# Seven block products in a decoder trunk: gate outputs in two tiles of one bank, value outputs in one tile of two banks

## The chip, the core and the metric

The kernel runs on one core of a Trainium2 chip, as one program. The metric is the device time of one execution in microseconds (us); of several runs the median is taken.

## What is computed

Two layers of a causal decoder over 256 positions of width 2048, in fp32. Layer 0 has stick-breaking attention, layer 1 dilated sliding-window attention; both have the same feed-forward block, where the change lies:

```python
def conv_ffn(h, w_up, conv_w, conv_b, w_down):
    u = causal_depthwise_conv(h @ w_up, conv_w, conv_b)     # width 3, along the positions
    gate, val = u[..., :D_FF], u[..., D_FF:]                # D_FF = 5632
    return (jax.nn.silu(gate) * val) @ w_down
...
for i in range(DEPTH):                                      # DEPTH = 2
    h = rms_norm(x, attn_norm_w[i])
    x = x + (mixer_a(...) if i < 1 else mixer_b(...))
    x = x + conv_ffn(rms_norm(x, ffn_norm_w[i]), ffn_w_up[i], ...)
    gate = jax.nn.sigmoid(rms_norm(x, ple_norm_w[i]) @ ple_w_gate[i])
    x = x + gate * (p[i] @ ple_w_proj[i])
return rms_norm(x, final_norm_w)
```

## The kernel before

**Matmuls.** Tokens are stationary (two tiles of 128), weights are the moving operand, 512 columns (a strip) at a time. Each operand is split into a high and a low part in a reduced fp32 format, and a block product is three matmuls: low tokens by high weights, high by low, high by high (`add_block`, lines 342 to 344). So a tile of weights, two blocks of 128 rows by 512 columns, gives 12 matmuls: two blocks, two token tiles, three matmuls.

**Weights.** `weights` loads four blocks (1 MB) at a time into `raw` (four buffers, SyncE's queue), then ScalarE (ACT) makes the high part `whi` of two blocks (line 305) and VectorE (DVE) the low part `wlo` (line 306). Four buffers of each are there, so the split runs up to four tiles ahead of TensorE (PE).

**Outputs in PSUM.** The eight banks of PSUM are dealt out by tag: "acc", a ring of five tiles of one bank; "att", one tile of one bank; "two", one tile of two banks. A strip's output is two banks, one for each token tile. `scaled` (line 540) copies them out on ScalarE, two transposes on VectorE (line 243) and a trip through memory (lines 246 and 254, GpSimd's queue) turn them, and the convolution runs on the turned strip (lines 905 to 914).

**Seven products.** In the up projection the strips come in pairs, each with a gate strip and a value strip. For every second pair, four of the 16 blocks of rows are taken out of the strips and made as one two by two block product (two token tiles by the gate and the value strip), with seven products instead of eight, ahead of the pair. `Seven` holds this: `load` fetches the two strips' weights, `first` to `seventh` each issue six matmuls (line 455) on weights that `parts` splits (lines 445 and 446). The outputs are four banks: c11 and c21 belong to the next gate strip (`strip_among` goes on accumulating into them), c12 and c22 to the next value strip. The first four products run between the weight tiles of the value strip before (`HEADS8`, `HEADS6`), the fourth ahead of its last tile. Then VectorE combines the outputs in place:

```python
def fourth(self):
    ...
    nc.vector.tensor_tensor(self.p, self.c22, self.p, op=OP.add)        # line 495
    nc.vector.tensor_tensor(self.c21, self.c21, self.p, op=OP.add)      # line 496
    nc.vector.tensor_tensor(self.c22, self.q, self.c21, op=OP.subtract) # line 497
    nc.vector.tensor_tensor(self.c12, self.c12, self.p, op=OP.subtract) # line 498
```

The other three products run within the next gate strip (`TAILS`): the fifth, into c11, ahead of its first weight tile; the sixth, into c21, ahead of the second; the seventh, into c12, ahead of the fourth. A weight tile gives six matmuls into the first bank, then six into the second. There are ten such blocks of seven: two and three in the two parts of each layer's feed-forward.

**What sets the order.** A scheduler places the instructions of each engine by priority and by its own estimate of time, and each engine then runs its list in order. It also sets the waits, and it tracks accesses by tile: an instruction that writes one bank of a tile of two banks waits for instructions that use the other. `high_priority` moves the weight splits and the combining steps forward in VectorE's and ScalarE's lists.

Of the kernel before, what the change touches and what calls it, by code (L numbers as in the profile page):

```python
# [75 lines left out]
def tile_trunk(ctx, tc, head_d, xT_d, x_d, pT_d, pos_d, vec_d, cst_d, csb_d, wqkv, wo_a, wkv, wq_b, wo_b, wup, wdn, wpg, wpp, gfin_d, out_d):  # L76
# [11 lines left out]
    def nm(s):  # L88
        uid[0] += 1
        return f"{s}_{uid[0]}"  # L90

    def bank(s, tag="att"):
        return psum.tile([P, 512], F32, tag=tag, bufs=NBANK[tag], name=nm(s))

    def two_banks():
        return psum.tile([P, 2, 512], F32, tag="two", bufs=1, name=nm("two"))
# [4 lines left out]
    def tt(s, shape=(P, S), dt=F32, tag=None, bufs=None):  # L101
        kw = {} if bufs is None else {"bufs": bufs}
        return tmp.tile(list(shape), dt, tag=tag or s, name=nm(s), **kw)
# [235 lines left out]
    def add_block(ps, x, t, hi, lo, first, final, again=False):  # L339
        xh = x[:, t * P : (t + 1) * P]  # L340
        xl = x[:, S + t * P : S + (t + 1) * P]
        nc.tensor.matmul(ps, xl, hi, start=first, stop=False, skip_group_check=again)  # L342
        nc.tensor.matmul(ps, xh, lo, start=False, stop=False, skip_group_check=again)  # L343
        nc.tensor.matmul(ps, xh, hi, start=False, stop=final, skip_group_check=again)  # L344
# [82 lines left out]
    class Seven:  # L427
# [36 lines left out]
            (self.b11, self.b21), (self.b12, self.b22) = ((r[:, :2], r[:, 2:]) for r in raws)  # L464

        def first(self):
            gates = two_banks()
            self.c11, self.c21 = gates[:, 0], gates[:, 1]
            self.c12, self.c22 = (bank("seven", "acc") for _ in range(2))
            both = tt("part", (P, 1024), tag="e", bufs=1)  # L470
            self.p, self.q = both[:, :512], both[:, 512:]
            w = self.parts(self.b11)
            self.t, self.u = self.b11, self.b12
            self.add(self.t, self.b11, self.b12)
            self.add(self.u, self.b12, self.b22)
            self.product(self.c11, self.token(0, 0), w, True)
            with tc.high_priority(offset=AHEAD):
                nc.scalar.activation(self.p, self.c11, AF.Copy)
# [162 lines left out]
    def stick_weights(q, k):  # L641
# [41 lines left out]
        return [ws[1 - h // 2][:, h % 2 * 3 : h % 2 * 3 + 3] for h in range(HG)]  # L683

    def mixer_a(xs, rc, first):
        ring_room = lambda: rt("u")
        rq = tt("rq", (P, 2), bufs=2)
# [502 lines left out]
```

## Time and profile before

| | |
|---|---|
| median of 3 runs | 2318.47 us (2317.86 to 2318.61) |
| the profiled execution | 2320.84 us, span from first to last instruction 2319.1 us |
| TensorE busy | 2285.9 us, 99% |
| VectorE busy | 1624.0 us, 70% |
| ScalarE busy | 1300.0 us, 56% |
| mean granted clock of TensorE | 0.993 |
| moved by DMA | 538.44 MB, mean 232 GB/s |

Shares are of the span. A matmul's row has the time from its start to its modelled end, drain included, so matmuls overlap: of two in a row the distance of the starts says what one costs. The granted clock is the share of full speed that TensorE was given. A name such as `two<-whi,h` reads: output tile, then the inputs.

### The profile page before, as it was taken

How to read it: one execution, taken by the hardware profiler on the slowest of the kernel's cores; microseconds unless marked ns; L12 is line 12 of the kernel's file. 1: busy time of each engine (PE TensorE's matmuls, PEld its weight loads, DVE VectorE, ACT ScalarE, POOL GpSimd, SP SyncE). 2: the span in 40 equal slices, each digit the busy share in tenths (PEclk: the TensorE clock that was granted, in tenths of full speed). 3: DMA queues.
4: the chain of work that ended last, by engine and by line, in shares of the span. 5: the costliest groups of instructions: out<-in, count | busy, mean ns of one | idle time of the engine just before them, and what ended most of it. 6: DMA issues, size and time to landing. Idle time of an engine off the chain costs nothing.

```text
span 2319.1 us, 27960 instructions
## 1 busy us (share of the span) xinstructions
PE 2285.9 (99%) x10137; PEld 1890.0 (81%) x10137; DVE 1624.0 (70%) x2335; ACT 1300.0 (56%) x1734; POOL 328.7 (14%) x575
## 2 busy tenths in 40 slices
PE   9999999999999999999999999999999999999998
PEld 7888888877888778788888888887788877878887
DVE  7666666788756788865677765778875578886565
ACT  6554555666534666645565554666653466664554
POOL 0211111111100111101011331211110011110100
PEclk9999999999999999999999999999999999999999
DMA  8877677676755767757676776768675577776763
GB/s 295 260 236 249 218 246 242 224 255 214 246 200 182 250 224 237 260 206 243 213 256 241 253 260 216 257 227 265 221 249 195 186 245 227 240 256 205 242 227 118
DMA packets 98347, 538.44 MB, mean 232 GB/s; under 512 B 16672, under 2 KB 17568, under 8 KB 46752
## 3 DMA queue, kind: packets, MB, share of 16 engines
q1 hardware_dynamic: 63360, 435.46, 54.2%
q0 software_dynamic: 32560, 95.98, 13.6%
q10 hardware_dynamic: 2288, 5.21, 0.6%
q8 instruction: 79, 1.29, 0.2%
q14 instruction: 60, 0.49, 0.1%
HBM read 486.52 MB, written 50.07 MB: 231 GB/s over the span
## 4 chain that ended last, share of the span: by engine, by line
PE 96%; DVE 2%; ACT 1%; DMA 1%; issue 0%; POOL 0%
PE accv L343 25%; PE accv L344 25%; PE accv L342 25%; PE two L342 3%; PE two L343 3%; PE two L344 3%; PE two L455 3%; PE seven L344 2%; PE seven L342 2%; PE seven L343 2%; PE two L554 1%; PE seven L455 1%; ACT whi L305 1%; DVE wlo L306 1%; DVE wlo L446 0%; DMA turned<-there 0%
## 5 line engine op out<-in xcount | busy, mean ns | idle before, releaser
L306 DVE TENSOR_TENSOR wlo<-raw,whi 128x1024 fp32r<-128x1024 f32 (+1 forms) x784 | 952.0, 1216 | 573.9 <-ACT whi L305 571.5
L305 ACT ACTIVATE whi<-raw 128x1024 fp32r<-128x1024 f32 (+1 forms) x784 | 825.7, 1054 | 808.2 <-PE accv L344 619.3
L342 PE MATMUL accv<-whi,h 128*128 128x512 f32 (+1 forms) x1688 | 655.6, 389 | 2.5 <-ACT whi L305 1.7
L344 PE MATMUL accv<-whi,h 128*128 128x512 f32 (+1 forms) x1688 | 657.0, 389 | 0.0
L343 PE MATMUL accv<-wlo,h 128*128 128x512 f32 (+1 forms) x1688 | 656.1, 389 | 0.0
L342 PEld LDWEIGHTS accv<-whi,h 128*128 128x128 f32 x1688 | 317.3, 188 | 68.6 <-ACT whi L305 2.2
L343 PEld LDWEIGHTS accv<-wlo,h 128*128 128x128 f32 x1688 | 317.3, 188 | 65.7 <-DVE wlo L306 0.4
L344 PEld LDWEIGHTS accv<-whi,h 128*128 128x128 f32 x1688 | 317.4, 188 | 64.8
L246 POOL DMA_DIRECT2D there<-y x162 | 91.7, 567 | 1300.2 <-DVE y L243 1282.4
L342 PE MATMUL accv<-whi,g 128*128 128x512 f32 x704 | 273.9, 389 | 0.0
L343 PE MATMUL accv<-wlo,g 128*128 128x512 f32 x704 | 273.9, 389 | 0.0
L344 PE MATMUL accv<-whi,g 128*128 128x512 f32 x704 | 273.9, 389 | 0.0
L254 POOL DMA_DIRECT2D turned<-there x324 | 190.1, 594 | 449.7 <-DMA there<-y 202.7
L343 PEld LDWEIGHTS accv<-wlo,g 128*128 128x128 f32 x704 | 132.2, 188 | 27.5
L342 PEld LDWEIGHTS accv<-whi,g 128*128 128x128 f32 x704 | 132.2, 188 | 27.5
L344 PEld LDWEIGHTS accv<-whi,g 128*128 128x128 f32 x704 | 132.2, 188 | 27.2
L445 ACT ACTIVATE whi<-raw 128x1024 fp32r<-128x1024 f32 x70 | 74.0, 1058 | 63.2 <-PE accv L344 35.5
L446 DVE TENSOR_TENSOR wlo<-raw,whi 128x1024 fp32r<-128x1024 f32 x70 | 85.5, 1221 | 26.3 <-ACT whi L445 26.3
L342 PE MATMUL two<-whi,h 128*128 128x512 f32 x240 | 96.1, 400 | 0.0
L343 PE MATMUL two<-wlo,h 128*128 128x512 f32 x240 | 95.5, 398 | 0.0
L344 PE MATMUL two<-whi,h 128*128 128x512 f32 x240 | 95.1, 396 | 0.0
L342 PE MATMUL seven<-whi,h 128*128 128x512 f32 x240 | 93.4, 389 | 0.0
(206 smaller groups left out, 2441.5 us busy)
## 6 DMA issues: line engine op xcount, KB each, us to landing
raw<-in_wup SPq DMA_DIRECT2D x176, 1024.0 KB, 5.4
raw<-in_wdn SPq DMA_DIRECT2D x88, 1024.0 KB, 5.0
there<-y POOLq DMA_DIRECT2D x171, 256.0 KB, 5.3
turned<-there POOLq DMA_DIRECT2D x324, 128.0 KB, 4.9
raw<-in_wqkv SPq DMA_DIRECT2D x40, 1024.0 KB, 6.0
raw<-in_wpg SPq DMA_DIRECT2D x32, 1024.0 KB, 4.9
raw<-in_wkv SPq DMA_DIRECT2D x24, 1024.0 KB, 5.3
raw<-in_wo_a SPq DMA_DIRECT2D x16, 1024.0 KB, 5.3
```

The source lines that it names most:

```text
L246: nc.gpsimd.dma_start(there[t * P : (t + 1) * P], y)
L254: nc.gpsimd.dma_start(z[32 * b : 32 * b + 32].rearrange("p a o r -> p a (o r)"), back[b])
L305: last["high"] = nc.scalar.activation(hi[:, c], r, AF.Copy).ins
L306: last["low weights"] = nc.vector.tensor_tensor(lo[:, c], r, f32(hi[:, c]), op=OP.subtract).ins
L342: nc.tensor.matmul(ps, xl, hi, start=first, stop=False, skip_group_check=again)
L343: nc.tensor.matmul(ps, xh, lo, start=False, stop=False, skip_group_check=again)
L344: nc.tensor.matmul(ps, xh, hi, start=False, stop=final, skip_group_check=again)
L445: last["high"] = nc.scalar.activation(hi, r, AF.Copy).ins
L446: last["low weights"] = nc.vector.tensor_tensor(lo, r, f32(hi), op=OP.subtract).ins
L455: nc.tensor.matmul(ps, x, y, start=begins, stop=ends, skip_group_check=True)
L554: run.append(nc.tensor.matmul(*args, skip_group_check=True, **kw).ins)
```

## The change

c11 and c21, the gate outputs, become two tiles of one bank: c11 in the bank of tag "att", c21 in the ring "acc". c12 and c22, the value outputs, become the tile of two banks, tag "two". Nothing else is edited.

```diff
         def first(self):
-            gates = two_banks()
-            self.c11, self.c21 = gates[:, 0], gates[:, 1]
-            self.c12, self.c22 = (bank("seven", "acc") for _ in range(2))
+            self.c11, self.c21 = bank("gates"), bank("gates", "acc")
+            values = two_banks()
+            self.c12, self.c22 = values[:, 0], values[:, 1]
```

TensorE's instructions keep their order, as do the queues of SyncE and GpSimd; only waits differ on TensorE, while VectorE's and ScalarE's lists change near the block products. The rows below are from the first block, and the others read the same. A number behind a name tells one tile from another; in brackets stand the engines and queues that a row waits for.

TensorE at the end of the value strip, before (the fifth product begins in the third row, with weights 3849 and 3850):

```order
L343 MATMUL accv_3618<-wlo_3798,h_3318 128x512
L344 MATMUL accv_3618<-whi_3797,h_3318 128x512
L455 MATMUL two_3641<-whi_3849,h_2700 128x512 [waits DVE_49,Activation_49]
L455 MATMUL two_3641<-wlo_3850,h_2700 128x512
L455 MATMUL two_3641<-whi_3849,h_2700 128x512
```

And now:

```order
L343 MATMUL accv_3618<-wlo_3798,h_3318 128x512
L344 MATMUL accv_3618<-whi_3797,h_3318 128x512
L455 MATMUL gates_3641<-whi_3849,h_2700 128x512 [waits Activation_49]
L455 MATMUL gates_3641<-wlo_3850,h_2700 128x512 [waits DVE_49]
L455 MATMUL gates_3641<-whi_3849,h_2700 128x512
```

Before, the first row of the product held a wait for VectorE that covered all that follows; now that row waits for ScalarE's high part alone and the second for the low part.

TensorE six matmuls later, now, in the first weight tile of the gate strip:

```order
L342 MATMUL gates_3641<-whi_3861,h_2862 128x512 [waits Activation_49]
L343 MATMUL gates_3641<-wlo_3862,h_2862 128x512 [waits DVE_49]
L344 MATMUL gates_3641<-whi_3861,h_2862 128x512
L342 MATMUL gates_3641<-whi_3861,h_2865 128x512
L343 MATMUL gates_3641<-wlo_3862,h_2865 128x512
L344 MATMUL gates_3641<-whi_3861,h_2865 128x512
L342 MATMUL gates_3642<-whi_3861,h_2862 128x512 [waits DVE_49]
```

The last row is the first write into c21 (`gates_3642`) after line 497 has read it; it has a wait of its own for VectorE, where the same row before had none.

VectorE around the combining steps, before:

```order
L495 TENSOR_TENSOR part_3644<-seven_3643,part_3644 128x512
L446 TENSOR_TENSOR wlo_3878<-raw_3619,whi_3877 128x1024
L496 TENSOR_TENSOR two_3641<-two_3641,part_3644 128x512
L498 TENSOR_TENSOR seven_3642<-seven_3642,part_3644 128x512
L497 TENSOR_TENSOR seven_3643<-part_3644,two_3641 128x512
L306 TENSOR_TENSOR wlo_3888<-raw_3859,whi_3887 128x1024
L243 STREAM_TRANSPOSE y_3818<-u_3813 128x4x4x32
```

And now:

```order
L495 TENSOR_TENSOR part_3644<-two_3643,part_3644 128x512
L446 TENSOR_TENSOR wlo_3878<-raw_3619,whi_3877 128x1024
L496 TENSOR_TENSOR gates_3642<-gates_3642,part_3644 128x512
L243 STREAM_TRANSPOSE y_3818<-u_3813 128x4x4x32
L497 TENSOR_TENSOR two_3643<-part_3644,gates_3642 128x512
L306 TENSOR_TENSOR wlo_3888<-raw_3859,whi_3887 128x1024
L498 TENSOR_TENSOR two_3643<-two_3643,part_3644 128x512
```

Line 498 went behind a weight split, and a transpose of the value strip before took its place ahead of line 497.

ScalarE where the block's value strip is evicted, before and then now:

```order
L305 ACTIVATE whi_4205<-raw_4203 128x1024
L540 ACTIVATE u_4131<-seven_3642,rcol_3055 128x512
L305 ACTIVATE whi_4221<-raw_4203 128x1024
L540 ACTIVATE u_4133<-seven_3643,rcol_3055 128x512
L905 ACTIVATE gate_4142<-turned_4024,vec 128x256 x3
```

```order
L305 ACTIVATE whi_4205<-raw_4203 128x1024
L305 ACTIVATE whi_4221<-raw_4203 128x1024
L540 ACTIVATE u_4131<-two_3643,rcol_3055 128x512
L540 ACTIVATE u_4133<-two_3643,rcol_3055 128x512
L905 ACTIVATE gate_4142<-turned_4024,vec 128x256 x2
```

The two evictions stood on either side of a weight split and now stand together behind it. At the gate strip it is the other way round.

## The prediction

> **What bounds the kernel now.** I read the busy shares first, then the waits of TensorE, then the instructions around the one wait that matters, engine by engine.
>
> ```profile
> PE 2285.9 (99%) x10137; PEld 1890.0 (81%) x10137; DVE 1624.0 (70%) x2335; ACT 1300.0 (56%) x1734; POOL 328.7 (14%) x575
> PE two L455 <- DVE seven L497: 19.6, 10, 2.0
> PE accv L342 <- ACT whi L305: 1.7, 1, 1.7
> SPq L288 <- DVE wlo L306: 1659.5, 341, 8.7
> ```
>
> The first line (the page's busy times) says that TensorE (PE) is the bound: 99%. The next two, from the list of who waited for whom (us in total, times, longest), say that almost all of its named waiting is one event that comes ten times, once for each block of seven products: a matmul of line 455 into the tile "two" waits 2.0 us for VectorE's (DVE) line 497. The last line says that the queue of weight loads waits for buffers to come free (1659.5 us in 341 waits): loads follow TensorE and do not hold it up. So the work elsewhere is cover, and only the ten places count.
>
> The timeline of TensorE at the first of them (start, duration, then the instruction; a duration includes the drain, so the pitch is read from start to start):
>
> ```profile
> 471.56 0.39 PE L344 MATMUL accv<-whi,h 128*128 128x512 f32 x1
> 473.91 0.47 PE L455 MATMUL two<-whi,h 128*128 128x512 f32 x1 [1.96 <-DVE seven L497]
> 475.36 0.60 PE L342 MATMUL two<-whi,h 128*128 128x512 f32 x1
> 475.76 0.63 PE L343 MATMUL two<-wlo,h 128*128 128x512 f32 x1
> 479.69 0.40 PE L455 MATMUL two<-whi,h 128*128 128x512 f32 x1
> ...
> 851.27 0.47 PE L455 MATMUL two<-whi,h 128*128 128x512 f32 x1 [1.96 <-DVE seven L497]
> 855.44 0.39 PE L455 MATMUL two<-whi,h 128*128 128x512 f32 x1
> ...
> 447.47 1.36 PE two L455 x6
> ```
>
> The last row, from the chain of work, gives the normal pitch: six matmuls in 1.36 us, 0.227 each. At 471.56 the value strip ends; the fifth product (into c11) should start at 471.79 and starts at 473.91. From there to the sixth product (479.69) lie 18 matmuls, 4.09 us at the normal pitch, but it takes 5.78 us: from 475.36 on the pitch is 0.40 to 0.43. At the fourth place the same 18 matmuls take 855.44 - 851.27 = 4.17 us. The windows from each of the ten waits' ends on (PE busy and matmuls, granted clock, DMA share, GB/s) say which places are of which kind:
>
> ```profile
> 473.90:479.50 5.60, 5.59 (x18) 0.70 0.96 332
> 563.40:569.00 5.60, 5.58 (x18) 0.70 0.95 332
> 761.70:767.30 5.60, 5.54 (x17) 0.70 0.98 335
> 851.20:856.80 5.60, 5.53 (x24) 1.00 0.98 345
> 939.10:944.70 5.60, 5.54 (x17) 0.70 0.96 343
> 1579.40:1585.00 5.60, 5.51 (x24) 1.00 0.97 340
> 1667.30:1672.90 5.60, 5.50 (x24) 1.00 0.95 336
> 1864.10:1869.70 5.60, 5.59 (x18) 0.70 0.90 337
> 1953.60:1959.20 5.60, 5.60 (x25) 1.00 0.97 334
> 2041.50:2047.10 5.60, 5.59 (x18) 0.70 0.91 336
> ```
>
> In six of ten the granted clock averages 0.70 and six matmuls fewer get through. A wait of 2 us is thus followed, more often than not, by a stretch at half clock.
>
> **What TensorE waits for.** VectorE and then ScalarE (ACT) at the same place:
>
> ```profile
> 467.09 1.22 DVE L446 TENSOR_TENSOR wlo<-raw,whi 128x1024 fp32r<-128x1024 f32 x1
> 469.00 1.23 DVE L306 TENSOR_TENSOR wlo<-raw,whi 128x1024 fp32r<-128x1024 f32 x1 [0.69 <-ACT whi L305]
> 470.14 0.68 DVE L495 TENSOR_TENSOR part<-seven,part 128x512 f32<-128x512 f32 x1
> 470.74 1.22 DVE L446 TENSOR_TENSOR wlo<-raw,whi 128x1024 fp32r<-128x1024 f32 x1
> 471.88 0.69 DVE L496 TENSOR_TENSOR two<-two,part 128x512 f32<-128x512 f32 x1
> 472.48 0.69 DVE L498 TENSOR_TENSOR seven<-seven,part 128x512 f32<-128x512 f32 x1
> 473.07 0.69 DVE L497 TENSOR_TENSOR seven<-part,two 128x512 f32<-128x512 f32 x1
> 473.67 1.22 DVE L306 TENSOR_TENSOR wlo<-raw,whi 128x1024 fp32r<-128x1024 f32 x1
> 474.81 1.30 DVE L243 STREAM_TRANSPOSE y<-u 128x512 f32<-128x512 f32 x2
> ...
> 465.25 1.06 ACT L445 ACTIVATE whi<-raw 128x1024 fp32r<-128x1024 f32 x1 [0.81 <-PE accv L344]
> 467.91 1.06 ACT L305 ACTIVATE whi<-raw 128x1024 fp32r<-128x1024 f32 x1 [1.60 <-PE accv L344]
> 470.63 0.69 ACT L540 ACTIVATE u<-accv,rcol 128x512 f32<-128x512 f32 x1 [0.25 <-PE accv L344]
> ```
>
> L497 computes c22 = q - c21: it reads the second bank of "two" and never touches c11, which the fifth product writes. The fifth product's own weights were ready long before: high part (L445) at 465.25 + 1.06 = 466.31, low part (L446) at 468.31. So it waits only because c11 and c21 are one tile. L497 ends at 473.76 and TensorE starts at 473.91: 0.15 us from the end to the start.
>
> **The change, part by part.**
>
> *The wait removed.* With c11 a tile of its own the fifth product has nothing left but its weights, so it starts at 471.79 instead of 473.91: 2.12 us. All ten waits are alike (19.6 over 10, longest 2.0), so 21.2 us. The restart (4.17 against 4.09 us at a place with full clock) goes with it: 0.08 x 10 = 0.8 us. The half clock follows only after the wait, in six places, and costs 5.78 - 4.17 = 1.61 us each: 9.7 us. Sum: 21.2 + 0.8 + 9.7 = 31.7 us, all of it on TensorE, which sets the end.
>
> [...]
>
> *The wait that is left.* c21 is still read by L497, and its next writer is no longer the fifth product but the second half of the first weight tile after it, 12 matmuls later (6 of the product, 6 into c11): 471.79 + 12 x 0.227 = 474.51. VectorE's order changes there: a transpose (L243) steps in between L496 and L497, and L498 falls behind the next weight split. The transpose takes half of the 1.30 us of its row of two, as L498 did (0.69), so L497 still ends at about 473.78, and TensorE may write at 473.93. That is 0.58 us early: no wait. The transpose needs the eviction L540, which ends at 471.32, 1.2 us before its new place (472.48). At nothing, therefore, but this cover is thin: each microsecond beyond 0.58 would cost ten.
>
> *The other products' weights.* The first tile after the fifth product has its halves by 468.97 (L305) and 470.23 (L306), and needs them at 473.15. The second tile's low part (L306 at 473.67, to 474.89) is needed after the sixth product, 24 matmuls on: 477.24. Early by 2.3 us. Later tiles are split as TensorE frees their buffers, so they move with it.
>
> *L498 behind a weight split.* It now ends near 475.5 instead of 473.17. c12 is next written by the seventh product, 48 matmuls after the fifth's start: 471.79 + 10.9 = 482.7. Covered by 7 us.
>
> *Evictions.* A tile is evicted as a whole: the gate halves, now apart, leave one after the other, and the value halves together:
>
> ```profile
> 511.18 0.69 ACT L540 ACTIVATE u<-seven,rcol 128x512 f32<-128x512 f32 x1 [0.30 <-PE seven L344]
> 513.57 0.67 ACT L540 ACTIVATE u<-seven,rcol 128x512 f32<-128x512 f32 x1
> ...
> 482.68 2.35 POOL L254 DMA_DIRECT2D turned<-there  x4 [5.72 <-ACT whi L305]
> turned<-there POOLq DMA_DIRECT2D x324, 128.0 KB, 4.9
> 498.33 1.08 ACT L905 ACTIVATE val<-turned,vec 128x256 f32<-128x256 f32 x2
> ```
>
> The first value half goes from 511.18 to 513.57 or so, 2.4 us later; the second, which ends the chain, stays within about 0.6 us. Behind it come transpose, a trip through memory and the convolution on ScalarE. For the value strip before it, the way back was issued at 482.68 to 485.03 and landed 4.9 us later (median), near 490; ScalarE used it at 498.33. That leaves 8 us, and still 4.5 when TensorE runs 3.8 us ahead. Costed at nothing, with that cover named; a gate strip's first half gains as much.
>
> *Banks.* A block takes one bank of the five-bank ring instead of two, and the bank that only the attention stages and the first norm use otherwise; nobody waited for either, so nothing is gained or lost.
>
> **Sum.** The profiled execution took 2320.84 us: 2320.84 - 31.7 = 2289.1. The median of the runs is 2318.47, 2.4 us less; the same sum gives 2286.8. How many of the ten waits fall into a half clock may differ from run to run: with four to eight instead of six the gain is 28.4 to 34.9.
>
> **Rivals.**
>
> *The wait moves to c21.* If anything delays VectorE's chain, TensorE stops at the first write of c21. One more weight split ahead of L497 is the natural size (470.74 to 471.88, 1.14 us): 1.14 - 0.58 = 0.56 us in each place, 5.6 in all, too short for the clock: 2292.4. For it: VectorE's order changes just there. Against: the operations in front of L497 sum to the same time. 0.10.
>
> *The half clock stays.* If the six stretches have another cause than the wait, only 22.0 us go: 2296.5. [...] Against: six of six lie right behind a wait. 0.05.
>
> *The change does nothing.* If the fifth product really waits for some other result that L497 happens to precede, the wait stays: 2318.5. Against: its weights' rows end 5.5 us before. 0.03.
>
> *Slower.* The value halves leave together, 2.4 us late; if all of that reaches TensorE at the next strip, with a half clock each time, it costs 2.4 + 1.61 + 0.08 = 4.1 us in ten places, 40.9 against 31.7: 2327.7. It makes the kernel measurably slower (0.2%, 4.6 us, is about what a measurement can tell from no change) only from a wait of 1.94 us per place on, every one with the half clock. Against: 8 us of cover. 0.02.
>
> **How the numbers follow.** The forecast has the remaining 0.80, 2287 with a range of its own from 2283.6 to 2290. The range reaches from the low end (eight half clocks) to just above the case in which the half clock stays: 2283.5 to 2297. Faster by over 0.2%: 0.80 + 0.10 + 0.05 = 0.95; within 0.2%: 0.03; slower: 0.02.
>
> **What would show it.** The row of TensorE waiting for L497 is gone or below 1 us in total; fifth products start 0.23 us behind the value strip's last matmul; granted clock 1.00 in all ten windows; c21's first write 12 matmuls later without idle time; value halves evicted in a pair. I am wrong if a wait for VectorE stands at the write of c21, if stretches at half clock remain where TensorE never paused, or if TensorE waits for weight splits in the strip after a block.

## The result, and the profile after

The changed kernel took 2287.58 us (median of 4 runs, 2286.19 to 2289.3) against 2318.54 for the kernel before beside it: a ratio of 0.9865, 95% interval 0.9848 to 0.9882. The forecast was 2287.0 with a range of 2283.5 to 2297. The profiled execution took 2287.39 us, with a span of 2285.6 against 2319.1. Of the ten executions of one experiment below, the delay with n = 1140, two took 4688 and 6498 us, for a reason that no trace shows; its median leaves them out.

First the busy times of the changed kernel (busy us, share of the span, instructions), then all that TensorE waited for by name (us in total, times, longest):

```profile
PE 2273.2 (99%) x10137; PEld 1882.0 (82%) x10137; DVE 1620.8 (71%) x2335; ACT 1298.6 (57%) x1734; POOL 327.7 (14%) x575
...
PE warm L125 <- DVE zero L122: 1.2, 1, 1.2
PE accv L342 <- DVE h L144: 0.9, 2, 0.7
PE accv L343 <- DVE wlo L306: 0.2, 1, 0.2
```

The row of ten waits for line 497 is gone and no other has come: 2.3 us of named waiting are left.

TensorE at the first block (start, duration): end of the value strip, the fifth product, its first weight tile, that tile's first write of c21, and the sixth product:

```profile
470.25 0.39 PE L344 MATMUL accv<-whi,h 128*128 128x512 f32 x1
470.47 0.39 PE L455 MATMUL gates<-whi,h 128*128 128x512 f32 x1
...
471.83 0.39 PE L342 MATMUL gates<-whi,h 128*128 128x512 f32 x1
...
473.19 0.39 PE L342 MATMUL gates<-whi,h 128*128 128x512 f32 x1
...
474.55 0.39 PE L455 MATMUL gates<-whi,h 128*128 128x512 f32 x1
```

The fifth product starts 0.22 us behind the value strip's last matmul, one pitch, and the sixth 4.08 us later: the normal pitch all the way. VectorE there:

```profile
470.56 0.69 DVE L496 TENSOR_TENSOR gates<-gates,part 128x512 f32<-128x512 f32 x1
471.16 0.70 DVE L243 STREAM_TRANSPOSE y<-u 128x512 f32<-128x512 f32 x1
471.79 0.67 DVE L497 TENSOR_TENSOR two<-part,gates 128x512 f32<-128x512 f32 x1
472.36 1.20 DVE L306 TENSOR_TENSOR wlo<-raw,whi 128x1024 fp32r<-128x1024 f32 x1
473.49 0.69 DVE L498 TENSOR_TENSOR two<-two,part 128x512 f32<-128x512 f32 x1
```

Line 497 still ends (472.46) nearly two microseconds after the fifth product's start (470.47), as it did before; now nobody stands behind it, since c21 is written 0.73 us after its end. So it is in nine places; in the sixth, near 1561, only 0.12 us are left, and TensorE hesitated there by less than 0.1.

Windows of the same 5.6 us from the fifth product's start, at the first and the sixth place (PE busy and matmuls, granted clock in the column behind POOL, DMA share, GB/s):

```profile
470.40:476.00 5.60, 5.60 (x27) 4.63 (x26) 5.60 (x9) 5.33 (x8) 0.57 (x1) 1.00 0.73 263
1558.10:1563.70 5.60, 5.60 (x26) 4.49 (x25) 5.60 (x8) 5.38 (x8) 0.57 (x1) 1.00 0.79 303
```

The clock is 1.00 in all ten, and 26 or 27 matmuls get through where it was 24 or 25 without a half clock and 17 or 18 with one.

The span became 33.5 us shorter, 1.8 more than the sum of 31.7. Of that, 1.31 us were there before the first block: the value strip's last matmul ahead of it starts at 470.25 instead of 471.56. They come from the first microseconds. The first matmuls of weights there, before (with a window behind them) and then after:

```profile
6.54 0.70 PE L342 MATMUL accv<-whi,h 128*128 128x512 f32 x2 [1.70 <-ACT whi L305]
...
7.50:11.20 3.70, 3.70 (x11) 2.86 (x10) 2.36 (x5) 2.07 (x5) 0.00 (x0) 0.54 0.99 368
```

```profile
5.39 0.70 PE L342 MATMUL accv<-whi,h 128*128 128x512 f32 x2 [0.68 <-DVE h L144]
```

In the profiled execution of before, TensorE waited 1.70 us there, started 1.15 us later, and a seventh stretch at half clock followed (0.54 in the window), which the prediction does not mention. By 20 us all this was worth 1.3 us. It does not come with the layout: the kernel below with only VectorE's order changed keeps the old one, and all that TensorE waited for line 305 in it is 0.2 us. The ten blocks together gave 33.5 - 1.3 = 32.2 us.

The medians differ by 2318.54 - 2287.58 = 31.0 us.

### The profile page after: what moved, and what is told of

The parts are those of the page before. It is cut to its first block, busy times and chain, and to the rows that moved or that the text cites. A ratio compares the mean times of both kernels' runs of the same rounds, so it can differ in the third digit from the quotient of the medians.

```text
span 2285.6 us, 27930 instructions
## 1 busy us (share of the span) xinstructions
PE 2273.2 (99%) x10137; PEld 1882.0 (82%) x10137; DVE 1620.8 (71%) x2335; ACT 1298.6 (57%) x1734; POOL 327.7 (14%) x575
## 4 chain that ended last, share of the span: by engine, by line
PE 99%; DMA 0%; ACT 0%; DVE 0%; issue 0%; POOL 0%; SPq 0%; ACTq 0%
PE accv L343 26%; PE accv L342 26%; PE accv L344 26%; PE two L343 3%; PE two L342 3%; PE two L344 3%; PE gates L342 2%; PE gates L343 2%; PE gates L455 2%; PE gates L344 2%; PE two L455 2%; PE two L554 1%; PE keys L554 0%; DMA raw<-in_wqkv 0%; DMA turned<-there 0%; ACT whi L305 0%
## 5 line engine op out<-in xcount | busy, mean ns | idle before, releaser
L342 PE MATMUL gates<-whi,h 128*128 128x512 f32 x240 | 93.4, 389 | 0.0
L344 PE MATMUL gates<-whi,h 128*128 128x512 f32 x240 | 93.4, 389 | 0.0
L343 PE MATMUL gates<-wlo,h 128*128 128x512 f32 x240 | 93.4, 389 | 0.0
L342 PE MATMUL two<-whi,h 128*128 128x512 f32 x240 | 93.4, 389 | 0.0
```

## Experiments

The theory: only the wait that c11 and c21 share counts, 2.1 us of stop in ten places, and a half clock of 1.61 us follows in some of them. The rivals: the gain comes from the value outputs' new place, or from VectorE's new order; or the half clock has a cause of its own.

### Each part of the change alone

On the kernel before, the gate outputs made two tiles, and the value outputs left in the ring:

```diff
-            gates = two_banks()
-            self.c11, self.c21 = gates[:, 0], gates[:, 1]
+            self.c11 = bank("gates")
+            self.c21 = two_banks()[:, 0]
```

> The gate outputs are two tiles (c11 in the bank of tag att, c21 alone in a tile of two banks), the value outputs stay two banks of the ring, as before. If the gain comes from taking c11 out of c21's tile (my theory), all of it is here: 2287, within 3 us, no wait for line 497. If it comes from the ring's relief or from the values' joint tile, this stays at 2318. If half comes from each, about 2302.

It took 2288.1 us (ratio 0.9874, 0.9857 to 0.989), and the row of ten waits is gone. This part alone has all of the gain.

On the kernel before, only a value output moved; the gate outputs stay one tile:

```diff
-            self.c12, self.c22 = (bank("seven", "acc") for _ in range(2))
+            self.c12, self.c22 = bank("seven"), bank("seven", "acc")
```

> The other half alone: the gates stay one tile of two banks, and a value output leaves the ring for the bank of tag att, so that a block takes one bank of the ring instead of two, as in the changed kernel. My theory: no gain, 2318 within 3 us, ten waits of 2.0 us for line 497. The theory that banks in the ring were short: 2287, or a part of the way.

It took 2317.73 us (1.0004, 0.9993 to 1.0015): no gain. On the kernel before, lines 497 and 498 put into the changed kernel's order, with the transpose ahead of line 497:

```diff
-                nc.vector.tensor_tensor(self.c22, self.q, self.c21, op=OP.subtract)
-                nc.vector.tensor_tensor(self.c12, self.c12, self.p, op=OP.subtract)
+                with tc.issue_after(nc.vector.tensor_tensor(self.c22, self.q, self.c21, op=OP.subtract).ins):
+                    nc.vector.tensor_tensor(self.c12, self.c12, self.p, op=OP.subtract)
```

> The tiles stay as before, and line 498 is made to follow line 497, so that a transpose steps in ahead of line 497 and VectorE's order is the changed kernel's at this place. My theory: the transpose takes as long as line 498 did, the wait stays, 2318 within 3 us. The theory that the new order on VectorE made the gain: 2287 or a part of the way.

It took 2317.16 us (0.9996, 0.9985 to 1.0007): no gain. TensorE's waits of these two, the value output's move and then the order:

```profile
PE two L455 <- DVE seven L497: 19.6, 10, 2.0
```

```profile
PE two L455 <- DVE seven L497: 19.7, 10, 2.0
```

Neither the new place of the value outputs nor the order takes the wait away, so neither is the cause.

### The wait removed in another way

On the kernel before, with c11 and c21 still one tile, the fourth product runs one weight tile earlier, so that VectorE's combining is over when the fifth comes:

```diff
-HEADS8, HEADS6, TAILS = (1, 3, 5, 7), (1, 2, 4, 5), (0, 1, 3)
+HEADS8, HEADS6, TAILS = (1, 3, 5, 6), (1, 2, 3, 4), (0, 1, 3)
```

> The tiles stay as before, but the fourth product is issued one weight tile (2.7 us) earlier, so that the combining steps end earlier. My theory: the wait is only late by 2.1 us, so the shared tile costs nothing or little then: line 497 should end at about 0.4 us after the fifth product could start, 2291, between 2286 and 2293, with the granted clock at 1.00. The theory that the tiles' layout itself matters (banks that are written and read at once): no gain, 2318.

It took 2287.6 us (0.9871, 0.9857 to 0.9886), as much as the change brings. The expected remainder of the wait did not come: VectorE's and TensorE's timeline at the first place show line 497 done at 470.03 and the fifth product on time.

```profile
469.34 0.69 DVE L497 TENSOR_TENSOR seven<-part,two 128x512 f32<-128x512 f32 x1
...
470.30 0.40 PE L455 MATMUL two<-whi,h 128*128 128x512 f32 x1
```

The 0.4 us of the expectation was a misreckoning: before, line 497 ended 1.97 us after the fifth product could start (473.76 against 471.79), and the fourth product came one weight tile, 2.72 us, earlier, which leaves no wait. Line 497 came 2.24 us earlier, not the whole 2.72, and that was enough by 0.27. So the shared tile as such costs nothing: it costs while a reader of one bank is late for a writer of the other.

### The wait put back at c21

If the wait is the cause, putting one of the same length back at c21 must bring the time back, with or without the half clock. On the changed kernel, a sum that nobody uses goes between lines 496 and 497 on VectorE (in these kernels' rows it is line 496 itself, and the step of line 496 stands on 495); its length n sets the delay (abridged: the line that makes the tile `pad` is left out):

```diff
-                nc.vector.tensor_tensor(self.c21, self.c21, self.p, op=OP.add)
-                nc.vector.tensor_tensor(self.c22, self.q, self.c21, op=OP.subtract)
+                a = nc.vector.tensor_tensor(self.c21, self.c21, self.p, op=OP.add).ins
+                with tc.issue_after(a): a = nc.vector.reduce_sum(self.pad, x[0][:, :n].unsqueeze(1).to_broadcast([P, 2, n]), axis=X).ins
+                with tc.issue_after(a): nc.vector.tensor_tensor(self.c22, self.q, self.c21, op=OP.subtract)
```

With n = 826:

> The changed kernel with one more VectorE operation (a sum over 1652 elements, about 1.8 us) between lines 496 and 497, where the transpose of 0.6 us stood. With the 0.58 us that I found in hand, TensorE should stop 0.6 us at the first write of c21, ten times: 6 us and no half clock, 2293.5. If no time is really in hand: 2300. If short waits bring the half clock too, up to 2303.

With n = 1140:

> The same with a sum over 2280 elements, about 2.4 us: a wait of 1.25 us in ten places. Without half clock 12.5 us, 2300. [...]

With n = 1570:

> The same with a sum over 3140 elements, about 3.3 us: a wait of 2.1 us in ten places, as long as the one before the change, but in the changed layout and at the write of c21. My theory (the half clock follows the wait): 21 us of waits, 1 of restarts and some six half clocks of 1.6, together 2319, as before the change. If the half clock had to do with the old layout: 2309 and granted clock 1.00.

They took 2309.81 us (0.9959, 0.9945 to 0.9972), 2316.9 (0.9988, 0.9978 to 0.9998) and 2325.88 (1.0028, 1.0013 to 1.0043): the expectations were missed by some 16, 17 and 7 us. Waits of TensorE with n = 826, and behind them one of ScalarE:

```profile
PE two L343 <- DVE wlo L306: 4.3, 6, 0.8
PE two L342 <- ACT whi L305: 3.5, 5, 1.1
...
ACT val L905 <- DMA turned<-there: 71.1, 12, 7.7
```

And the same ScalarE row of the changed kernel:

```profile
ACT val L905 <- DMA turned<-there: 0.7, 1, 0.7
```

VectorE with n = 826, past the first block:

```profile
473.82 0.68 DVE L497 TENSOR_TENSOR two<-part,gates 128x512 f32<-128x512 f32 x1
474.41 1.22 DVE L306 TENSOR_TENSOR wlo<-raw,whi 128x1024 fp32r<-128x1024 f32 x1
...
478.71 1.23 DVE L306 TENSOR_TENSOR wlo<-raw,whi 128x1024 fp32r<-128x1024 f32 x1
479.85 1.30 DVE L243 STREAM_TRANSPOSE y<-u 128x512 f32<-128x512 f32 x2
```

With the sum in the list the scheduler placed both transposes behind four weight splits (the first and the last are shown), at 479.85 instead of 471.16 and 475.22. ScalarE, which runs its list in order, stood still at the convolution for up to 7.7 us until the turned strip came, and the weight splits behind it came late for TensorE. So these three kernels measure two things at once and cannot size the wait.

### The same, with the transposes held in place

On the changed kernel, the transposes get the priority that the weight splits have:

```diff
-                    there = turn_out(scaled(next(ups), rc, room))
+                    us = scaled(next(ups), rc, room)
+                    with tc.high_priority(offset=AHEAD): there = turn_out(us)
```

> The changed kernel with the two transposes of each up-projection strip given the priority of the weight splits, as the base of the next two. They leave at most 1.2 us earlier than in the changed kernel, and nobody waited for them there: 2287 within 2 us.

2287.86 us (0.9867, 0.985 to 0.9884): nothing gained or lost, so it serves as the base for the delays. With the sum of n = 826 in it:

> That base with the sum over 1652 elements (1.86 us) between lines 496 and 497. If the excess of the first runs with a delay came from transposes that fell behind four weight splits, so that ScalarE waited for the turned strip (71 us in 12 waits for line 905), then without that only the stop at c21 is left: 0.6 us in ten places, 2293.5, between 2291 and 2296. If the excess came from the added work itself, it stays near 2310.

2290.58 us (0.9881, 0.9866 to 0.9896): the 20 us that the same sum had cost without the priority (2309.81 - 2290.58 = 19.2) were the late transposes. What remains, 2.7 us (2290.58 - 2287.86), is 0.27 per place. VectorE and TensorE at the first one:

```profile
470.32 1.86 DVE L496 TENSOR_REDUCE pad<-x 128x2 f32<-128x1652 f32 x1
472.10 0.69 DVE L497 TENSOR_TENSOR two<-part,gates 128x512 f32<-128x512 f32 x1
...
472.12 0.39 PE L344 MATMUL gates<-whi,h 128*128 128x512 f32 x1
472.35 0.99 PE L342 MATMUL gates<-whi,h 128*128 128x512 f32 x2
473.18 0.40 PE L343 MATMUL gates<-wlo,h 128*128 128x512 f32 x1
```

Line 497 ends at 472.79, and the first write of c21 (the second of the two matmuls in the row from 472.35) starts 0.05 later, 0.26 us behind its normal place. I had expected 0.6. Two things make the difference. I had put 0.15 us between the two, 0.10 too much. And in all kernels with the sum the scheduler had moved one matmul of line 342 from later in the strip ahead of the first write of c21 (the first of the two in the row from 472.35), which gave line 497 one more pitch, 0.23 us.

With n = 1570:

> The same with the sum over 3140 elements (3.4 us): a wait of 2.1 us at c21 in ten places, as long as the one before the change. If wait and half clock go together whatever the layout: 21.4 of waits, 0.8 of restarts, and five or six half clocks of 1.6 us, as the kernels with ten waits of 2.0 us have shown: 2317 to 2319.5. If a half clock needs the old layout: 2309.

2307.09 us (0.9949, 0.9934 to 0.9963), some 10 us below the expectation. Its waits of TensorE, and the window behind the first of them:

```profile
PE gates L342 <- DVE two L497: 16.5, 10, 1.7
...
474.40:480.00 5.60, 5.49 (x24) 4.57 (x25) 5.60 (x8) 2.21 (x3) 1.48 (x3) 1.00 0.48 167
```

Ten waits of 1.65 us, and the granted clock is 1.00 behind all ten. The 19.2 us over 2287.86 are the waits and restarts alone: 1.92 a place. Ten waits of 1.65 us, then, cost their own time and no clock. This result separates the two terms of the sum.

With n = 1719, which makes the wait exactly as long as it was in the kernel before:

> The sum now over 3438 elements, so that TensorE's idle time at c21 should be listed with 1.96 us in place of 1.65, exactly as before the change. In all kernels so far a wait of 1.65 us brought no half clock (19 places) and one of 1.96 five or six in ten. If the length alone decides, in any layout: 22.7 us of waits and restarts on 2287.9, and five or six half clocks of 1.6: 2318.6 to 2320.2. If the half clock needs the old layout: 2310.6 and granted clock 1.00.

2318.99 us (1.0007, 0.9995 to 1.0019), as expected: the kernel before's time is back, from the changed layout. Its waits, and the windows from the first, the second and the last of its ten places on:

```profile
PE gates L342 <- DVE two L497: 19.6, 10, 2.0
...
475.90:481.50 5.60, 5.50 (x17) 0.70 0.51 173
565.50:571.10 5.60, 5.55 (x24) 1.00 0.49 167
...
2042.50:2048.10 5.60, 5.55 (x17) 0.70 0.56 178
```

Five of the ten windows read 0.70 like the first and the last, five read 1.00 like the second. From 1.65 to 1.96 us of wait, 3.1 us more in all, the time rose by 11.9: the half clocks make the rest, 8.8 us, and five of them at 1.61 are 8.1. The DMA share in the five windows with a half clock is 0.50 to 0.56 here, against 0.90 or more in the windows of before; and before, four windows at 0.95 or more had the full clock. So the DMA load isn't what calls for the half clock.

With n = 2031, a wait of 2.6 us:

> The sum over 4062 elements, an idle time of 2.6 us in ten places. Waits and restarts 29.3 us: 2317.2 without half clock. [...] If the length between 1.65 and 1.96 us is a sharp bound, all ten are hit: 2333.

2322.58 us (1.002, 1.001 to 1.0029), between the 2317.2 without a half clock and the 2333 with ten. The waits of 26.1 us were there, but in the profiled execution only two of ten places had a half clock (0.70 at the first, 0.74 at the third). It was the fastest of the ten, 2317.95 us; the median is 4.6 us longer, which at 1.61 each would be about three more half clocks, but those executions have no trace. Why a longer wait can be followed less often than a shorter one, the last section says.

## Why the prediction was right, point by point

*The wait removed (22.0 us with the restart).* Right, and shown both ways: the row is gone when only c11 and c21 are parted, and the time is back when a wait of the same length is put back. The waits of 1.65 us, which cost 1.92 per place, size it: from start to start TensorE took 2.04 us there instead of 0.23, 1.81 more, and the matmuls behind it lost another 0.13 (at the first place the six behind the wait took 1.49 us instead of 1.36), which makes 1.94. The same steps gave 2.12 + 0.08 for the kernel before. In the profiled executions the ten blocks gained 32.2 us together, against the 31.7 of the sum.

*The half clocks (9.7 us).* Right in kind: all six went with the wait, and they return with one of the same length. That they follow "only after the wait" was too narrow: the last section shows stretches behind other waits. Their number depends on the run, five to six in the profiles with a wait of 1.96 us, within the four to eight of the text. With n = 1719, 1.96 us of wait brought a half clock in five of ten places; with n = 1570, 0.31 us less of wait, the clock was 1.00 in all ten.

*The wait that is left at c21.* Right, by a little: 0.58 us of cover were forecast, 0.73 were measured in nine places. The 0.58 is the 0.73 less the 0.15 us that the step put between the end of VectorE and the start of TensorE, as at the fifth product; with the sum of n = 826 it was 0.05 at c21. Why it is shorter there, no run here shows. The rival's 5.6 us for one more weight split was twice what a like delay cost: the sum with n = 826 is 1.2 us longer than the transpose that it displaced, and cost 2.7 us, for the two reasons given there. That its 0.56 us would be "too short for the clock" agrees with the runs: behind waits of 1.65 us the clock was 1.00 in all ten places.

*Line 498, weights, evictions.* Right. TensorE has no row of waiting for the later weight tiles beyond the 0.2 us above. The value halves leave as a pair, and the gate halves apart (ScalarE of the changed kernel):

```profile
489.71 0.69 ACT L540 ACTIVATE u<-gates,rcol 128x512 f32<-128x512 f32 x1 [0.25 <-PE gates L344]
492.10 0.67 ACT L540 ACTIVATE u<-gates,rcol 128x512 f32<-128x512 f32 x1
...
508.42 1.25 ACT L540 ACTIVATE u<-two,rcol 128x512 f32<-128x512 f32 x2
```

The pair's late first half reached nobody: the convolution of a value strip waited once, for 0.7 us.

*The rivals.* The wait at c21, the half clock that stays and the change that does nothing are each against a row above. The slower one had the right path, a late strip that reaches TensorE through ScalarE's order: the three delays without the priority took it, with another cause. Its price of 4.1 us per place is not what such a delay cost: with n = 826 the late transposes lost 2309.81 - 2290.58 = 19.2 us over ten places, 1.9 each.

*The sum.* 31.7 forecast, 31.0 between the medians. Wait, half clocks and cover were each as forecast, so the mechanism was right. That 2287.0 lies 0.6 from the result is in part luck: the half clocks vary from run to run, worth 1.61 us each.

## What to carry to other kernels

Where the bound engine's largest named wait ends on an operation that touches neither its inputs nor its output, look whether the two share a tile: tracking is by tile, and splitting the tile or finishing the operation earlier were worth the same here (2288.1 and 2287.6 us). Before pricing an added or a moved instruction by its own length, see what the scheduler then puts behind what: one sum of 1.86 us cost 2.7 us with the transposes held in place and 22 without. And look at the clock behind a stop of TensorE before you price it by its length: from 1.65 to 1.96 us, 0.3 us more of wait per place, the time rose by 12 us instead of 3, because half clocks came with it.

## What the runs showed that I had not expected

The prediction took the half clock for something that follows a 2 us wait "more often than not". The traces show more. In the trace of before the six stretches at half clock behind the ten waits begin at 475.37, 564.11, 762.09, 939.58, 1864.59 and 2042.08, and each lasts 3.41 us: the window from 475.37 to 478.78 has a clock of 0.50, the one from there to 564.11 has 1.00, and so at the others. The beginnings lie on one grid, 26, 58, 52, 271 and 52 steps apart, of (2042.08 - 475.37) / 459 = 3.413 us each. The first stretch of that execution, at 7.74, is 137 such steps ahead. A short window laid across a border gives its place, since the clock in it is a mean of 1 and 0.5. Here are one before and then one with n = 1719, with TensorE's write of c21 at the ninth place of that kernel:

```profile
475.30:475.40 0.10, 0.10 (x2) 0.83 1.35 573
```

```profile
1865.80:1865.90 0.10, 0.10 (x2) 0.72 0.00 0
...
1954.62 0.50 PE L342 MATMUL gates<-whi,h 128*128 128x512 f32 x1 [1.96 <-DVE two L497]
```

The first border lies at 475.37, the second at 1865.84, and so another at 1954.59, 26 steps on.

Of the waits of 1.96 us, those were followed by a stretch that lie whole in one step. In the kernel before, the six that do so were followed, and the four that a border of the grid cuts (1.70, 1.62, 1.51 and 1.18 us in the larger part) were not. With n = 1719 the five whole ones were followed, and five cut ones were not; of these, the one that ends at 1954.62 is cut by 0.03 us, with 1.93 left. The kernels with only a value output moved and with only the order changed have five whole waits each, all followed, and five cut ones, none followed. The ten waits of 1.65 us were never followed. Among all these waits, then, the longest part in one step that was not followed had 1.93 us, and the shortest that was had 1.96.

The block of products isn't needed for it. In the kernel with only the order changed, TensorE once waited 2.3 us for a transfer in the attention of layer 1, and the step from 1367.15 on was at half clock:

```profile
PE two L554 <- DMA turned<-there: 2.3, 1, 2.3
...
1367.15:1370.56 3.41, 3.41 (x13) 0.50 0.01 2
```

Idle time between rows isn't the whole measure, though. One stretch followed a step with less of it: the one at 7.74 in before came behind a wait of 1.70 us, which itself came behind the kernel's warm-up matmuls (line 125). What else counts, no run here shows.

The grid explains the profiled execution with the wait of 2.6 us as well: only at two places did more than 1.93 us fall into one step (2.61 and 2.13); at the others the border left 1.90 or less on either side. On average the longer wait should be followed more often. If the grid lay by chance, and some 1.95 us in one step were needed, the longer one would be followed in (3.41 - 2.61 + 2 x (2.61 - 1.95)) / 3.41 = 62% of places, against 43% for 1.96 us: an estimate of mine from the measured step of 3.41 us and the waits above. Two of ten is how this execution lay on the grid. At the third place the half clock began while TensorE was still waiting (windows of that kernel: the wait, the step at half clock, and after):

```profile
759.90:762.40 2.50, 0.37 (x2) 0.00 (x0) 2.50 (x2) 2.01 (x5) 0.00 (x0) 1.00 0.64 269
762.40:765.80 3.40, 2.92 (x7) 2.34 (x8) 3.40 (x6) 0.00 (x0) 1.13 (x2) 0.50 0.21 80
765.80:769.00 3.20, 3.20 (x16) 2.63 (x15) 2.92 (x3) 2.12 (x2) 1.10 (x2) 1.00 0.90 289
```

What places the grid against a program's start, and so how many of ten equal waits are hit, no run here shows.
